# Moving the pre-work of the branch weights inside a hybrid mLSTM, attention and MLP layer, and the second branch's merges from GpSimd to VectorE

## The chip, the cores and the metric

The kernel runs on one core of a Trainium2 chip. The metric is the device time of one execution in microseconds (us), the median of several runs. Engines are named as in the profile: PE is TensorE, DVE is VectorE, ACT is ScalarE, POOL is GpSimd, and SP is the engine whose queue issues nearly all of this kernel's DMA transfers.

## The reference, cut to what matters

One decoder layer over 1024 positions of width 1024, in fp32. Three branches (mLSTM, differential attention, attention into 256 memory tokens) work on the normed input, each is projected back to 1024 columns and weighted by a gate, and the weighted sum goes through an output projection and an MLP.

```python
h = rms_norm(x, norm_mix_g[l])
proj = h @ w_in[l]
mq, mk, mv, mi, mf, mo, dq, dk, dv, cq = jnp.split(proj, split_idx, axis=-1)
qk = jax.nn.silu(causal_depthwise_conv(jnp.concatenate([mq, mk], axis=-1), conv_w[l], conv_b[l]))
mq, mk = jnp.split(qk, 2, axis=-1)
hm = mlstm_chunkwise(...)                # 4 heads of 128 x 256, chunks of 128 positions
y_m = jax.nn.sigmoid(mo) * rms_norm(hm, ...)
y_d = diff_attention(...)
y_c = memory_cross_attention(...)
g_m, g_d, g_c = jnp.split(jax.nn.sigmoid(h @ w_gate[l] + b_gate[l]), N_BRANCH, axis=-1)
merged = g_m * (y_m @ w_proj_m[l]) + g_d * (y_d @ w_proj_d[l]) + g_c * (y_c @ w_proj_c[l])
x = x + merged @ w_out[l]
h2 = rms_norm(x, norm_mlp_g[l])
x = x + jnp.square(jax.nn.relu(h2 @ w_up[l])) @ w_down[l]
```

## The kernel before

Every fp32 operand of a large product is split into a high and a low half of the matmul's own format, and each product is three matmuls. Splitting a tile is a cast (ACT) and a subtraction (DVE, lines 117 to 129). The gates, the branch projections and the MLP's first product are Winograd (Strassen) products: seven products of quarter size in place of eight, for which sums of the quarters of both operands are formed first.

The stages, in the order in which PE runs them (span times of the profile before): the input norm and the memory branch to about 190 us; the mLSTM stream to 560; differential attention to 1142; the gates to 1216.5; the three branch projections to 1456; the output projection to 1544; the MLP's up-projection and then its down-projection to the end.

**The mLSTM stream** is eight head halves (head 3 to 0, two halves of 512 positions each), a list of steps in which PE always has a projection to compute. A head half's own steps are: projection of q and k with the causal conv's four taps on DVE (lines 674, 678, 681; tiles `pre`, `cv`), values `va`, output gate `tho`, the mask tile `ngb` loaded and turned into a weight matrix `mpT`, then four chunks (`C` is the state, `Ch` its split for the next chunk's scores, `den` the denominators) and `final`, which scales the heads' output (`hS`, line 794) and transposes it. The chunks of one half run while the next half's q and k are being projected.

`early()` weaves extra work into that list, by positions: the sums of the branch projections' weights that the Winograd products want (tile `es`). `sums` is four DVE operations of 128x512 and four stores (to `ws`, or from the branch input `y` to `xc_d`); `pairs` is four DVE operations of 128x256, seven splits (an ACT cast and a DVE subtraction each) and seven stores to `wh`. Each first loads its four tiles. There are 8 pairs and 12 sums. Before, three sums stand at the stream's start, and from position 112 on pair and sums alternate every 49 positions, so that they fall anywhere in a head half, which is 64 positions long.

**The branch projections** (`branches()`) are 3 branches of 28 steps (7 products p of 4 steps kp), 12 matmuls each. The input of a step is split 5 steps ahead (tile `xs`), its weight is loaded 9 steps ahead (for the third branch from `wh`, already split). At the end of a product four PSUM tiles are evicted, partly through `te`, multiplied by a gate tile `gl` (loaded from `gates` in DRAM) and merged: branch 1 makes `mg`, branch 2 adds into `mg`, branch 3 adds `mg` and keeps the split result for the output projection. POOL does the merges of branch 2 (line 1611), part of those of branch 3 (line 1614), and sums and differences of the input's rows (`row`).

**Output projection and up-projection.** The output projection has four groups of four outputs; each output gets its residual in one DVE operation (line 1775, into a `gl` tile), is stored, and is squared into `ssq` by ACT and POOL (line 1782) for the next norm. It is also scaled (ACT, `h`) and stored to `h_d`, from where the up-projection loads its input `xr` in four parts `X[0]` to `X[3]`, forms the quarter sums (`xts`, lines 1274 to 1277) and splits them (`xo`). Its weights come as `wraw`, with sums by POOL (lines 1292 to 1295), and are split into `wo`.

The order on each engine is set by a scheduler at build time; `issue_after` and `behind` are hints to it that put an instruction behind another one without a semaphore. `self.hold` is such a mark for the first `wraw` loads.

Of the kernel before, what the change touches and what calls it, by code (L numbers as in the profile page):

```python
# [19 lines left out]
S = 1024  # L20
# [53 lines left out]
class Layer:  # L74
# [1249 lines left out]
    def wino(self, ws, load, use, first, parts):  # L1324
# [13 lines left out]
        X[2] = self.wino_x(2, load)  # L1338
# [91 lines left out]
    def early(self, pool, add):  # L1430
# [24 lines left out]
        def sums(p, srcs, dst, x):  # L1455
            t = []
            flat = lambda q: f32(q.rearrange("p a b -> p (a b)"))

            def load():
                t.extend(flat(new()) for _ in range(4))  # L1460
                return [nc.sync.dma_start(o, s) for o, s in zip(t, srcs)]

            def calc():
                t.extend([flat(new())] + ([None] * 2 if x else [t[1], t[2]]))
                return four(t, x)

            def store():
                r0, r1, r2, r3, e, f, g = t
                return [nc.sync.dma_start(dst[i], o) for i, o in enumerate((r0, r2, e, r3) if x else (r0, f, e, g))]

            at(p, load)
            at(p + 8, calc)
            at(p + 12, store)

        def pairs(p, b, kp, h):
# [19 lines left out]
            at(p, load)  # L1495
            at(p + 8, calc)
            for i in range(7):
                at(p + 10 + i, lambda i=i: cut(i))
                at(p + 13 + i, lambda i=i: keep(i))
# [3 lines left out]
        p = 2  # L1503
        for _ in range(3):
            sums(p, *S.pop(0))
            p += 17
        p = 112
        for n in range(8):
            pairs(p, 1, n // 2, n % 2)
            p += 29  # L1510
            sums(p, *S.pop(0))
            p += 20
        sums(p, *S.pop(0))
# [5 lines left out]
    def branches(self, pools, fetch, hi, lo):  # L1519
# [37 lines left out]
        def split(n, f):  # L1557
# [13 lines left out]
            if bi and p < 2:  # L1571
                r = lambda i: rows[bi, i, kp]
                if p == 0:
                    G.tensor_sub(r(1), r(2), r(0))
                else:
                    G.tensor_sub(r(3), r(3), r(1))

# [6 lines left out]
        def sums(bi, kp):  # L1584
            r = lambda i: rows[bi, i, kp]
            if bi == 1:
                t = op.tile([P, 512], F32, tag=("sq", "h2")[kp % 2], name=self.name("row"))
            else:
                t = xd.tile([P, 512], F32, tag="mh", name=self.name("row"))
            rows[bi, 4, kp] = t  # L1590
            G.tensor_sub(t, r(2), r(0))
            G.tensor_sub(r(0), r(0), r(1))
# [4 lines left out]
        def gate():  # L1597
            if outs:
                gates.append(fetch(self.gdr, *outs.pop(0)))

        mg, T, S = {}, {}, {}

        def out(bi, u, m, hf, c, late):
# [5 lines left out]
            elif bi == 1:  # L1609
                V.scalar_tensor_tensor(out=t, in0=t, scalar=1.0, in1=c, op0=ALU.add, op1=ALU.mult)  # L1610
                G.tensor_add(mg[ft, hf], mg[ft, hf], t)
            else:
# [3 lines left out]
                def keep():  # L1616
# [3 lines left out]
                    gate()  # L1620

                return keep
            gate()

        def evict(bi, p, u, ps):
# [7 lines left out]
            elif p in (1, 4):  # L1633
                V.tensor_add(T[u], T[u], ps)
                return out(bi, u, *((0, 1) if p == 1 else (1, 0)), T[u], False)
# [16 lines left out]
        for n in range(N):  # L1652
# [22 lines left out]
            for f in todo.pop(n, []):  # L1675
                k = f()
                if k:
                    if n < N - 1:
                        todo.setdefault(n + 2, []).append(k)
                    else:  # L1680
                        k()
# [11 lines left out]
        for n in sorted(todo):  # L1693
            for f in todo[n]:
                f()
        self.pinned = False
        self.hold = self.mark
# [25 lines left out]
    def tail(self):  # L1723
# [5 lines left out]
        def fetch(d, f, hf):  # L1729
            t = gls.tile([P, 512], F32, tag="gl", name=self.name("gl"))  # L1730
            nc.sync.dma_start(t, half(d, f, hf))
# [3 lines left out]
        with ExitStack() as c0:  # L1735
# [9 lines left out]
            with ExitStack() as c1:  # L1745
                E = lambda *x, **k: c1.enter_context(tc.tile_pool(*x, **k))
                self.pmm, self.kmm, self.nmm = Banks(E, "pmm2"), 8, 3
                if True:
# [10 lines left out]
                    V.memset(hole[:, 0:1], 0.0)  # L1759
                    V.memset(gap[:, 0:1], 0.0)  # L1760
# [8 lines left out]
                    for g in range(4):  # L1769

                        def res(m, hf, ps):
# [3 lines left out]
                            V.scalar_tensor_tensor(out=x, in0=ps, scalar=0.5, in1=x, op0=ALU.mult, op1=ALU.add)  # L1775
# [12 lines left out]
                        self.group(w, lambda k, i, hf: (lo if i else hi)[self.WOUT[k], hf], res, g == 0)  # L1788

# [446 lines left out]
```

## Time and profile before

| | |
|---|---|
| median of 3 runs | 2178.77 us (2174.14, 2178.77, 2179.9) |
| profiled execution | 2178.04 us, of which the span is 2176.2 |
| mean granted PE clock | 0.995 |
| busy: PE | 2117.4 us, 97% of the span |
| busy: DVE, ACT, POOL | 1556.2, 1055.3, 642.2 us |
| memory read and written | 214.15 MB and 98.60 MB, 144 GB/s over the span |

PE is busy nearly all the time, so what can be gained or lost in a change of order is PE's idle time, 58.8 us, and the time in which its clock is halved. A row of the profile names the line, the engine and the operation with its output and inputs; for a wait it names the instruction that ended it.

### The profile page before, as it was taken

What the parts mean: (1) busy time and instruction counts of PE and PEld (TensorE: products, weight loads), DVE (VectorE), ACT (ScalarE), POOL (GpSimd) and SP (SyncE); (2) the same over time, 40 slices, a digit from 0 to 9 for tenths busy, and PEclk for the clock granted to TensorE, in tenths of its full rate; (3) what the DMA queues carried; (4) which work ended last, traced back from release to release, by engine and by line L of the source; (5) the groups of instructions that cost most, each with busy time, mean ns of one, the idle gap of its engine ahead of it and who ended that gap; (6) DMA issues with size and microseconds to landing.
All of it is one profiled execution on the core that took longest, in us unless ns stands there. A gap on an engine that the chain in (4) does not pass through costs nothing.

```text
span 2176.2 us, 31507 instructions
## 1 busy us (share of the span) xinstructions
PE 2117.4 (97%) x10905; PEld 1829.7 (84%) x10905; DVE 1556.2 (72%) x2953; ACT 1055.3 (48%) x2183; POOL 642.2 (30%) x776
## 2 busy tenths in 40 slices
PE   7999999999999999999999999999899999999999
PEld 5888888888899999999887787788688888888887
DVE  6644677686647777777666588774578888876698
ACT  6543355454336666666554445334444544643331
POOL 2100000000111111111113054622455577665562
PEclk9999999999999999999999999999899999999999
DMA  6116456655343333333343885656434544844443
GB/s 242 42 67 207 132 190 211 198 184 174 138 154 90 86 86 89 90 95 88 97 150 112 300 273 158 228 194 220 136 112 150 208 155 156 294 161 154 159 160 107
DMA packets 183207, 340.00 MB, mean 156 GB/s; under 512 B 17633, under 2 KB 52742, under 8 KB 180998
## 3 DMA queue, kind: packets, MB, share of 16 engines
q1 hardware_dynamic: 176710, 318.05, 45.6%
q10 hardware_dynamic: 6336, 19.93, 2.3%
q8 instruction: 86, 1.41, 0.3%
q14 instruction: 75, 0.61, 0.1%
HBM read 214.15 MB, written 98.60 MB: 144 GB/s over the span
## 4 chain that ended last, share of the span: by engine, by line
PE 77%; DVE 9%; DMA 7%; ACT 2%; issue 2%; POOL 1%; SPq 0%; DVEq 0%; ACTq 0%; POOLq 0%
PE mm L96 30%; PE p L96 28%; PE mm L1668 7%; PE sc L96 5%; PE po L96 3%; PE tp L101 3%; DMA xr<-h_d 1%; DMA es<-in_wq 1%; DVE w L126 1%; DVE xs L69 1%; DVE cv L678 1%; DVE w L69 1%; DVE es L1451 1%; DMA raw<-in_wd 1%; PE pr L101 1%
## 5 line engine op out<-in xcount | busy, mean ns | idle before, releaser
L96 PE MATMUL mm<-w,hT 128*128 128x384 f32 (+3 forms) x2496 | 472.8, 332 | 5.7 <-DVE va L126 2.4
L96 PE MATMUL mm<-hT,w 128*128 128x512 f32 x1680 | 408.2, 393 | 0.3 <-ACT gt L503 0.3
L96 PEld LDWEIGHTS mm<-w,hT 128*128 128x128 f32 x2496 | 391.5, 190 | 17.2 <-DVE va L126 2.8
L96 PEld LDWEIGHTS mm<-hT,w 128*128 128x128 f32 x1680 | 308.2, 188 | 60.7 <-ACT gt L503 0.9
L96 PE MATMUL p<-xo,wo 128*128 128x512 f32 x1344 | 309.0, 392 | 1.6 <-DVE gl L1775 1.6
L96 PE MATMUL p<-xd,wo 128*128 128x512 f32 x1344 | 305.1, 389 | 0.0
L96 PEld LDWEIGHTS p<-xo,wo 128*128 128x128 f32 x1344 | 253.7, 189 | 55.6 <-DVE gl L1775 2.0
L96 PEld LDWEIGHTS p<-xd,wo 128*128 128x128 f32 x1344 | 252.2, 188 | 52.7 <-DVE acc L69 0.4
L1668 PE MATMUL mm<-xs,w 128*128 128x512 f32 x1008 | 231.4, 391 | 8.2 <-DMA w<-wh 4.7
L1668 PEld LDWEIGHTS mm<-xs,w 128*128 128x128 f32 x1008 | 190.0, 189 | 49.5 <-issue 5.1
L117 ACT CAST wo<-wraw 128x896 fp32r<-128x896 f32 x124 | 117.0, 944 | 230.2 <-PE p L96 87.3
L69 DVE TENSOR_TENSOR wo<-wraw,wo 128x896 fp32r<-128x896 f32 x124 | 148.5, 1209 | 47.0 <-ACT wo L117 47.0
L1292 POOL TENSOR_TENSOR wraw<-wraw 128x128 f32<-128x128 f32 x128 | 98.2, 767 | 229.9 <-DMA wraw<-in_wdown 95.2
L1041 ACT ACTIVATE dpe<-sc,dst,drr 128x256 f32<-128x256 f32 (+7 forms) x128 | 106.6, 833 | 97.0 <-DVE dst L1037 95.8
L126 DVE TENSOR_TENSOR w<-raw,w 128x256 fp32r<-128x256 f32 (+4 forms) x257 | 127.6, 521 | 28.1 <-ACT w L124 27.5
L124 ACT CAST w<-raw 128x256 fp32r<-128x256 f32 (+4 forms) x257 | 116.3, 488 | 48.2 <-PE mm L96 12.1
L151 POOL TENSOR_SCALAR hss<-hss 128x4 f32<-128x4 f32 x8 | 6.1, 765 | 429.7 <-ACT mscr L785 429.7
L1033 DVE CUSTOM_DVE_ANT_0 sc<-sc,tmask 128x256 f32<-128x256 f32 (+7 forms) x128 | 97.1, 759 | 13.1 <-PE sc L96 12.3
L151 POOL TENSOR_SCALAR drr<-drr 128x16 f32<-128x16 f32 x16 | 3.3, 204 | 311.8 <-DVE drr L988 289.8
L1294 POOL TENSOR_TENSOR wraw<-wraw 128x128 f32<-128x128 f32 x128 | 92.8, 725 | 0.0
L96 PE MATMUL sc<-dk,dq 128*128 128x512 f32 (+3 forms) x384 | 91.9, 347 | 0.0
L69 DVE TENSOR_TENSOR acc<-acc,p 128x512 f32<-128x512 f32 x121 | 80.1, 684 | 15.8 <-PE p L96 15.1
(333 smaller groups left out, 3496.9 us busy)
## 6 DMA issues: line engine op xcount, KB each, us to landing
dk<-dsg SPq DMA_DIRECT2D x64, 256.0 KB, 4.0
wraw<-in_wup SPq DMA_DIRECT2D x64, 256.0 KB, 3.1
r_d<-xts SPq DMA_DIRECT2D x16, 1024.0 KB, 4.5
wraw<-in_wdown SPq DMA_DIRECT2D x64, 256.0 KB, 3.1
wh<-es SPq DMA_DIRECT2D x56, 256.0 KB, 2.6
w<-wh SPq DMA_DIRECT2D x28, 512.0 KB, 4.1
raw<-in_wd SPq DMA_DIRECT2D x32, 384.0 KB, 3.3
gl<-gates SPq DMA_DIRECT2D x48, 256.0 KB, 3.4
```

The costliest lines, as they stand in the source:

```text
L69: return self.tc.keep_in_program_order(f(*a, **k))
L96: ins = self.nc.tensor.matmul(out, l, r, start=start, stop=stop)
L101: self.pin(self.nc.tensor.transpose(out, x, self.ident))
L117: self.cast = self.A.copy(hi, src).ins
L124: a = nc.scalar.copy(hi, src)
L126: return a, nc.vector.tensor_sub(lo, src, f32(hi))
L678: V.scalar_tensor_tensor(out=c, in0=x[:, q : q + 512], scalar=cw(q), in1=c, op0=ALU.mult, op1=ALU.add)
L1033: V.tensor_tensor_reduce(out=sc[:, 0:n], in0=sc[:, 0:n], in1=self.tmask[:, D - n : D], scale=1.0, scalar=-3.0e38, op0=ALU.add, op1=ALU.max ...
L1041: nc.scalar.activation(pe[c][:, 0:n], sc[:, 0:n], AF.Exp, bias=t8[:, 2 + c : 3 + c], scale=rr[:, i, c : c + 1], accum_out=t8[:, 4 + c : 5 ...
L1292: G.tensor_add(r[:, 4], r[:, 0], r[:, 3])
L1294: G.tensor_sub(r[:, 6], r[:, 1], r[:, 0])
L1668: nc.tensor.matmul(cur[u], w[:, l, c], x[:, m], start=first and i == 0, stop=last and i == 2, skip_group_check=True)
```

## The change

The work is the same, but for two DVE memsets that are dropped; where it is done differs.

1. `early()`: the pair of each head half comes at position 42 of the half, between its taps and its values' use (its loads 8 or 16 positions ahead). From the third head half on, two sums per half follow at 60 and 71 positions (the second one stands beside the first chunks of the half, at position 7 of the next). No sums are left at the start of the stream or in the first two head halves.
2. `branches()`: the 16 merges of branch 2 and the 4 of branch 3's product 1 go from POOL to DVE. The row sums on POOL are formed in another way, with as many operations, four of which come later. The load of a gate tile is issued a step later, and hinted behind the mark.
3. The up-projection's first `wraw` load is held until the output projection's second group (before: until the end of the branch projections), and the DVE part of `X[2]` is hinted behind the last residual operation of the output projection.

```diff
@@ early
             at(p, load)
-            at(p + 8, calc)
-            at(p + 12, store)
+            at(p + q, calc)
+            at(p + r, store)
...
-            at(p, load)
-            at(p + 8, calc)
+            at(p - (16 if p > 124 else 8), load)
+            at(p, calc)
             for i in range(7):
-                at(p + 10 + i, lambda i=i: cut(i))
-                at(p + 13 + i, lambda i=i: keep(i))
+                at(p + 1 + i, lambda i=i: cut(i))
+                at(p + 4 + i, lambda i=i: keep(i))
...
-        p = 2
-        for _ in range(3):
-            sums(p, *S.pop(0))
-            p += 17
-        p = 112
-        for n in range(8):
+        for n, p in enumerate((106, 124, 202, 266, 330, 394, 458, 522)):
             pairs(p, 1, n // 2, n % 2)
-            p += 29
-            sums(p, *S.pop(0))
-            p += 20
-        sums(p, *S.pop(0))
+            if n >= 2:
+                sums(p + 10, 8, 11, *S.pop(0))
+                sums(p + (22 if n < 7 else 18), 7, 9, *S.pop(0))
@@ branches
-            if bi and p < 2:
+            if bi and p < 3:
                 r = lambda i: rows[bi, i, kp]
                 if p == 0:
-                    G.tensor_sub(r(1), r(2), r(0))
-                else:
+                    G.tensor_add(r(1), r(1), r(4))
+                elif p == bi:
                     G.tensor_sub(r(3), r(3), r(1))
+                elif p == 1:
+                    G.tensor_sub(r(0), r(2), r(1))
...
             G.tensor_sub(t, r(2), r(0))
-            G.tensor_sub(r(0), r(0), r(1))
+            if bi == 1:
+                G.tensor_sub(r(0), r(0), r(1))
...
                 gates.append(fetch(self.gdr, *outs.pop(0)))
+                self.behind(self.fetched, self.mark)
...
-                G.tensor_add(mg[ft, hf], mg[ft, hf], t)
+                V.tensor_add(mg[ft, hf], mg[ft, hf], t)
...
-                return out(bi, u, *((0, 1) if p == 1 else (1, 0)), T[u], False)
+                return out(bi, u, *((0, 1) if p == 1 else (1, 0)), T[u], p == 1)
...
-                    todo.setdefault(n + 2, []).append(k)
+                    todo.setdefault(n + (1 if k is gate else 2), []).append(k)
...
-        self.hold = self.mark
@@ wino (up-projection)
-        X[2] = self.wino_x(2, load)
+        with self.tc.issue_after(self.last_stt):
+            X[2] = self.wino_x(2, load)
@@ tail
-                    V.memset(hole[:, 0:1], 0.0)
-                    V.memset(gap[:, 0:1], 0.0)
...
+                        if g == 1:
+                            self.hold = self.mark
```

PE's order is the same in both kernels. Three places show how the other orders move (numbers behind names are the program's; lines of the changed kernel are its own, 1452 for 1451, 1771 for 1775).

DVE in the sixth head half, before: the end, with the sums of `y` between the taps' last operations and `hS`.

```order
L681 SCALAR_TENSOR_TENSOR cv_5266<-cth_5271,cv_5266 128x512
L126 TENSOR_TENSOR w_6005<-raw_6003,w_6005 128x256
L1451 TENSOR_TENSOR es_5335<-es_5294,es_5292 128x512
L126 TENSOR_TENSOR kh_5274<-cv_5266,kh_5274 128x512
L1451 TENSOR_TENSOR es_5292<-es_5292,es_5293 128x512
L126 TENSOR_TENSOR va_1833<-mm_5320,va_1833 128x256
L1451 TENSOR_TENSOR es_5294<-es_5294,es_5292 128x512
L1451 TENSOR_TENSOR es_5295<-es_5295,es_5294 128x512
L794 TENSOR_SCALAR hS_5102<-hS_5102,hss_5103 128x256 x4
```

Before `hS` are four sums and, for the first of them, the landing of a load from `y`. The same stretch in the changed kernel:

```order
L126 TENSOR_TENSOR va_1832<-mm_5224,va_1832 128x256
L126 TENSOR_TENSOR w_5276<-raw_5274,w_5276 128x256
L794 TENSOR_SCALAR hS_5052<-hS_5052,hss_5053 128x256
L681 SCALAR_TENSOR_TENSOR cv_5213<-cth_5218,cv_5213 128x512
L794 TENSOR_SCALAR hS_5052<-hS_5052,hss_5053 128x256 x3
L126 TENSOR_TENSOR kh_5221<-cv_5213,kh_5221 128x512
L126 TENSOR_TENSOR w_5295<-raw_5274,w_5295 128x256
L126 TENSOR_TENSOR va_1833<-mm_5259,va_1833 128x256
```

The four `es` operations ahead of `hS` are gone. They stand earlier now, beside the first chunks of the same half, the last of the first sums and the first of the second:

```order
L1452 TENSOR_TENSOR es_4925<-es_4925,es_4924 128x512
L725 TENSOR_TENSOR ngb_5447<-ngb_5447,tmaskT 128x512
L126 TENSOR_TENSOR w_5046<-raw_5044,w_5046 128x256
L126 TENSOR_TENSOR w_5085<-raw_5044,w_5085 128x256
L773 SCALAR_TENSOR_TENSOR C_5064<-C_4653,g_dec,sc_5054 128x258
L126 TENSOR_TENSOR Ch_5066<-C_5064,Ch_5066 128x258
L781 TENSOR_TENSOR den_5069<-den_5069,g_col 128x1
L782 RECIPROCAL den_5069<-den_5069 128x1
L1452 TENSOR_TENSOR es_5091<-es_5030,es_5029 128x512
L773 SCALAR_TENSOR_TENSOR C_5106<-C_5064,g_dec,sc_5096 128x258
L1452 TENSOR_TENSOR es_5029<-es_5029,es_5032 128x512
L126 TENSOR_TENSOR Ch_5108<-C_5106,Ch_5108 128x258
```

Here the first `es` operation of the second sums (`es_5091`) stands ahead of the second chunk's `C`, and waits for loads that SP issues behind the four stores of the first sums. Before, a pair's subtractions (line 1489) stood around the first chunk's `C`:

```order
L1489 TENSOR_TENSOR es_4995<-es_4995 128x256
L773 SCALAR_TENSOR_TENSOR C_5114<-C_4704,g_dec,sc_5104 128x258
L1489 TENSOR_TENSOR es_5060<-es_5060 128x256
L126 TENSOR_TENSOR Ch_5116<-C_5114,Ch_5116 128x258
L781 TENSOR_TENSOR den_5119<-den_5119,g_col 128x1
L1489 TENSOR_TENSOR es_5061<-es_5061 128x256
L782 RECIPROCAL den_5119<-den_5119 128x1
L1489 TENSOR_TENSOR es_5062<-es_5062 128x256
L773 SCALAR_TENSOR_TENSOR C_5161<-C_5114,g_dec,sc_5151 128x258
L126 TENSOR_TENSOR Ch_5163<-C_5161,Ch_5163 128x258
```

The subtractions needed no load; the sums in their place do. POOL in the middle of branch 2, before: merges (line 1611) between sums of rows (lines 1574 and 1576).

```order
L1611 TENSOR_TENSOR mg_14424<-mg_14424,gl_15044 128x512
L1611 TENSOR_TENSOR mg_14429<-mg_14429,gl_15049 128x512
L1574 TENSOR_TENSOR row_14577<-row_14887,row_14787 128x512
L1611 TENSOR_TENSOR mg_14455<-mg_14455,gl_15074 128x512
L1611 TENSOR_TENSOR mg_14460<-mg_14460,gl_15079 128x512
L1574 TENSOR_TENSOR row_14600<-row_14909,row_14809 128x512
L1574 TENSOR_TENSOR row_14623<-row_14931,row_14831 128x512
L1574 TENSOR_TENSOR row_14649<-row_14957,row_14857 128x512
L1611 TENSOR_TENSOR mg_14527<-mg_14527,gl_15150 128x512
L1611 TENSOR_TENSOR mg_14531<-mg_14531,gl_15155 128x512
L1576 TENSOR_TENSOR row_14679<-row_14679,row_14577 128x512
```

Eight merges stand between the row operations that branch 3 needs. In the changed kernel, where the merges are on DVE:

```order
L1569 TENSOR_TENSOR row_14621<-row_14621,row_15081 128x512
L1569 TENSOR_TENSOR row_14647<-row_14647,row_15127 128x512
L1573 TENSOR_TENSOR row_14829<-row_14929,row_14621 128x512
L1573 TENSOR_TENSOR row_14855<-row_14955,row_14647 128x512
L1571 TENSOR_TENSOR row_14677<-row_14677,row_14571 128x512
L1571 TENSOR_TENSOR row_14699<-row_14699,row_14598 128x512
L1571 TENSOR_TENSOR row_14721<-row_14721,row_14621 128x512
L1571 TENSOR_TENSOR row_14749<-row_14749,row_14647 128x512
L1613 TENSOR_TENSOR gl_15488<-mg_14314,gl_15488 128x512
```

POOL has only the row operations left, up to the first merge of branch 3 (line 1613).

DVE at the end of the output projection, before: the three `xts` operations of `X[2]` stand ahead of three residual operations and the splits of two weights (`wo`).

```order
L1775 SCALAR_TENSOR_TENSOR gl_16396<-mm_16371,gl_16396 128x512
L1274 TENSOR_TENSOR xts_16681<-xr_16679 128x512
L1276 TENSOR_TENSOR xts_16681<-xr_16679,xts_16681 128x512
L1277 TENSOR_TENSOR xts_16681<-xr_16679,xts_16681 128x512
L1775 SCALAR_TENSOR_TENSOR gl_16431<-mm_16406,gl_16431 128x512
L1775 SCALAR_TENSOR_TENSOR gl_16466<-mm_16441,gl_16466 128x512
L126 TENSOR_TENSOR wo_16697<-wraw_16661,wo_16697 128x7x128
L69 TENSOR_TENSOR wo_16734<-wraw_16691,wo_16734 128x7x128
L1775 SCALAR_TENSOR_TENSOR gl_16501<-mm_16476,gl_16501 128x512
```

The residual operations behind them wait for `xr`, the landing of `X[2]`. In the changed kernel:

```order
L1771 SCALAR_TENSOR_TENSOR gl_16394<-mm_16369,gl_16394 128x512
L1771 SCALAR_TENSOR_TENSOR gl_16429<-mm_16404,gl_16429 128x512
L1771 SCALAR_TENSOR_TENSOR gl_16464<-mm_16439,gl_16464 128x512
L126 TENSOR_TENSOR wo_16695<-wraw_16659,wo_16695 128x7x128
L69 TENSOR_TENSOR wo_16732<-wraw_16689,wo_16732 128x7x128
L1771 SCALAR_TENSOR_TENSOR gl_16499<-mm_16474,gl_16499 128x512
L1274 TENSOR_TENSOR xts_16679<-xr_16677 128x512
L126 TENSOR_TENSOR xo_16684<-xr_16677,xo_16684 128x3x512
L1276 TENSOR_TENSOR xts_16679<-xr_16677,xts_16679 128x512
L1277 TENSOR_TENSOR xts_16679<-xr_16677,xts_16679 128x512
```

All four residual operations of the last group now stand ahead of `X[2]`.

More of the change, by code (lines that the diff above doesn't have):

```diff
@@ L1453, in early, with sums @@
         new = lambda: pool.tile([P, 2, 256], F32R, tag="w", name=self.name("es"))
-        def sums(p, srcs, dst, x):
+        def sums(p, q, r, srcs, dst, x):
             t = []
@@ L1619, in keep @@
                     self.split2(hi[ft, hf], lo[ft, hf], t)
-                    gate()
+                    return gate
                 return keep
-            gate()
+            return gate
         def evict(bi, p, u, ps):
@@ L1676, in branches @@
                 k = f()
+                while k and n == N - 1:
+                    k = k()
                 if k:
-                    if n < N - 1:
-                        todo.setdefault(n + 2, []).append(k)
-                    else:
-                        k()
+                    todo.setdefault(n + (1 if k is gate else 2), []).append(k)
             if n + LEAD < N + 4:
@@ L1694, in branches @@
             for f in todo[n]:
-                f()
+                while f:
+                    f = f()
         self.pinned = False
-        self.hold = self.mark
         return w0
@@ L1730, in fetch @@
             t = gls.tile([P, 512], F32, tag="gl", name=self.name("gl"))
-            nc.sync.dma_start(t, half(d, f, hf))
+            self.fetched = nc.sync.dma_start(t, half(d, f, hf)).ins
             return t
@@ L1774, in res @@
                             x = fetch(a["xT"], f, hf)
-                            V.scalar_tensor_tensor(out=x, in0=ps, scalar=0.5, in1=x, op0=ALU.mult, op1=ALU.add)
+                            self.last_stt = V.scalar_tensor_tensor(
+                                out=x, in0=ps, scalar=0.5, in1=x, op0=ALU.mult, op1=ALU.add
+                            ).ins
                             nc.sync.dma_start(half(self.x1d, f, hf), x)
```

## The prediction

> **What bounds the kernel now.** I read the profiled execution first by engine, then by stage, then by PE's waits in each stage.
>
> ```profile
> PE 2117.4 (97%) x10905; PEld 1829.7 (84%) x10905; DVE 1556.2 (72%) x2953; ACT 1055.3 (48%) x2183; POOL 642.2 (30%) x776
> 190.00:560.00 370.00, 353.69 (x2081) 311.34 (x2080) 260.71 (x685) 180.42 (x510) 13.86 (x14) 0.99 0.58 189
> 1216.50:1456.00 239.50, 231.26 (x1009) 190.04 (x1008) 187.49 (x229) 104.04 (x186) 95.72 (x65) 0.99 0.69 229
> 1456.00:1544.00 88.00, 87.16 (x385) 71.84 (x385) 44.65 (x55) 32.32 (x47) 27.12 (x21) 1.00 0.64 208
> 1544.00:1562.00 18.00, 9.18 (x40) 7.18 (x38) 11.01 (x10) 8.46 (x10) 9.26 (x8) 0.82 0.46 157
> ```
>
> The last four rows are stretches of the span: length, then busy time of PE, its weight loads, DVE, ACT and POOL, then PE's granted clock. PE bounds everything; PE's order does not change, so the change can only give back or add PE's idle time and the time at a lower clock. Length less busy PE is 16.3 us of idle in the mLSTM stream, 8.2 in the branch projections, 0.8 in the output projection, 8.8 at the up-projection's start: 34.1 us within reach of the change. The other 24.7 of PE's 58.8 idle us lie at the start, in attention, the gates and the MLP, which it does not touch.
>
> The clock comes on top. Four stretches ran at half clock; behind two of them I put one of equal length just after:
>
> ```profile
> 453.16:456.57 3.41, 3.41 (x18) 3.41 (x18) 3.17 (x9) 0.00 (x0) 0.00 (x0) 0.50 0.91 224
> 457.50:460.91 3.41, 3.41 (x31) 3.36 (x30) 2.98 (x7) 1.69 (x5) 0.00 (x0) 1.00 0.77 270
> 500.95:504.36 3.41, 3.41 (x17) 3.25 (x17) 1.21 (x4) 1.09 (x2) 0.00 (x0) 0.50 0.59 190
> 1391.83:1395.24 3.41, 3.41 (x8) 2.69 (x9) 0.00 (x0) 0.00 (x0) 0.50 (x1) 0.50 0.96 365
> 1397.00:1400.41 3.41, 3.41 (x17) 2.83 (x16) 1.30 (x2) 0.68 (x2) 0.00 (x0) 1.00 0.73 215
> 1555.67:1569.32 13.65, 8.70 (x29) 7.45 (x29) 5.11 (x4) 6.87 (x10) 11.83 (x19) 0.50 0.60 200
> ```
>
> 18 matmuls where 31 fit: 13/31 of 3.41 us lost, 1.4 us. The second, by the same pace, 1.4. The third 9/17 of 3.41, 1.8. The fourth did 29 in 8.70 busy us; at 17 in 3.41 it would have done 43, so 14/43 of 8.70, 2.8 us. Together 7.4 us.
>
> **The mLSTM stream: what goes.** PE's waits there:
>
> ```profile
> PE tp L101 <- DVE hS L794: 7.3, 4, 4.4
> PE mm L96 <- DVE va L126: 2.4, 2, 1.8
> ...
> PE sc L96 <- ACT Ch L124: 1.9, 2, 1.5
> ...
> PE sc L96 <- DVE Ch L126: 1.0, 3, 0.4
> ```
>
> Columns: total us, times, longest. DVE's own order shows who stands ahead at the longest `hS` and `va`:
>
> ```profile
> 449.51 0.76 DVE L1489 TENSOR_TENSOR es<-es 128x256 fp32r<-128x256 f32 x2
> ...
> 451.45 0.42 DVE L126 TENSOR_TENSOR va<-mm,va 128x256 fp32r<-128x256 f32 x1
> ...
> 496.79 0.69 DVE L1451 TENSOR_TENSOR es<-es,es 128x512 f32<-128x512 f32 x1 [1.73 <-DMA es<-y]
> ...
> 498.94 1.41 DVE L1451 TENSOR_TENSOR es<-es,es 128x512 f32<-128x512 f32 x2
> 500.26 1.14 DVE L794 TENSOR_SCALAR hS<-hS,hss 128x256 f32<-128x256 f32 x4
> ```
>
> At `hS` it is 1.73 us of waiting for a load and four sums, 2.8 us: 4.5, about the 4.4 us that PE stood. So `es` operations in DVE's queue make the stalls. In the changed order none stand before the third head half except two pairs, and later none between the taps and `hS`. I count 15.3 of the 16.3 us as gone (1.0 kept for the short `Ch` waits) and the two half-clock stretches, 2.8: 18.1 us.
>
> The clock needs a rule here, since both stretches follow a stall within 3 to 5 us. The first comes after a stall of 1.8 us, the row of `va`. The Trainium skill, "TensorE: Matmul & The Clock Gate", section "Why this matters for your kernels", asks only that PE have no idle gap over about 3 us; by it the first stretch would not be there, and this trace disagrees. By that page new stalls under 3 us would cost no clock; the sum would not move, as I charge them none either.
>
> **The mLSTM stream: what comes in.** The pair at position 42 has only `tho` and splits around it, before values are needed 14 positions later; seven subtractions and four sums are 11 x 0.4 us (the rows at 449.51 and 451.45 show that size), spread over as many positions: hidden. Its loads are put ahead on SP, where the mask tile `ngb` is queued; DVE waits for that tile before the change too. The first sums stand after `mpT`, ahead of nothing that PE needs soon: hidden too. The second sums are the price. Their four loads sit on SP behind the four stores of the first sums, and their first operation stands ahead of the second chunk's `C` on DVE, on which `Ch` and PE's next scores hang.
>
> ```profile
> L1461 SPq DMA_DIRECT2D es<-in_wq x32: 422/430/686, 194.4 to 420.5; - x32
> L1469 SPq DMA_DIRECT2D ws<-es x32: 319/327/1014, 201.7 to 428.6; - x32
> DMA to landing us min/median/max: 2.0/3.4/6.8
> DVE es L1451 <- DMA es<-in_wq: 7.7, 7, 2.8
> ```
>
> From the end of the first sums: four stores at 0.33, two loads at 0.43 and a landing of 3.4 make 5.6 us until the first operation can run (4.2 with the shortest landing, 9.0 with the longest). The stream's 370 us for eight halves make a head half at most 46 us and a position of 64 at most 0.7; the second chunk follows the first by 4 positions, 2.8 us, and the first sums end about a position ahead of the first chunk, so DVE is there 3 to 4 us after them. It then waits about 2 us (0 to 5.5). How much of it reaches PE the trace does not show. Below it is nothing; above, the nearest row is the 4.4 us at `hS`, where a 1.73 us wait met the end of a full queue. Here one 0.68 us operation and not four stands between, and `Ch` has a chunk's 2.8 us to run in, so I take 1.2 us per half, nearer to zero. Six halves have such sums: 7.2 us (0 to 26). Net gain in the stream 10.9.
>
> **The branch projections.** PE's waits, and what SP waits for:
>
> ```profile
> PE mm L1668 <- DMA w<-wh: 4.7, 1, 4.7
> PE mm L1668 <- DVE xs L69: 2.0, 2, 1.7
> PE mm L1668 <- DVE hole L1759: 1.6, 1, 1.6
> SPq L1731 <- POOL mg L1611: 36.0, 16, 6.1
> 1379.61 3.52 POOL L1611 TENSOR_TENSOR mg<-mg,gl 128x512 f32<-128x512 f32 x2
> 1379.61 7.49 DVE L69 TENSOR_TENSOR xs<-row,xs 128x512 fp32r<-128x512 f32 x5
> ```
>
> The weight that came late was queued on SP behind gate loads (line 1731), which wait for a `gl` tile that POOL's merge still reads, and POOL was behind with merges and row sums. With the merges on DVE right behind the multiplication, and the load a step later, that wait (4.7 and its 1.8 of clock) goes. The `xs` waits (2.0) have the other half of the cause: beside POOL, DVE's splits took 1.5 us each (7.49 for five) where the sums above take 0.68. Less POOL work means faster splits. The 1.6 us at the stage's start stay: there DVE is busy with the last gate's sums, and dropping a memset takes away a name, not the work. Gain 4.7 + 1.8 + 2.0 = 8.5 us.
>
> The price is 20 additions on DVE, 20 x 0.68 = 13.6 us on an engine that is busy 187.5 of 239.5 us; against that, 20 POOL operations of about 1.7 us no longer slow the splits. I cost it at nothing; the cover is the five steps of lead, 12 matmuls each: 239.5 us / 84 = 2.85 us a step, 14 us.
>
> The Trainium skill, "SBUF — State Buffer", section "SBUF: two separate sides", says that DVE and GpSimd share a port pair as an exclusive lock: a DVE operation with two SBUF inputs is blocked while a GpSimd one holds it. The rows above (1.5 against 0.68 us) agree. By it the new DVE merges, which have two SBUF inputs, would be caught too wherever POOL still sums rows; that is the slower rival below, worked out from rows there.
>
> **The output projection's end.**
>
> ```profile
> 1537.86 7.65 DMA xr<-h_d
> ...
> 1545.60 0.69 DVE L1274 TENSOR_TENSOR xts<-xr 128x512 f32<-128x512 f32 x1 [12.99 <-DMA xr<-h_d]
> 1545.64 1.80 POOL L1275 TENSOR_TENSOR xts<-xr 128x512 f32<-128x512 f32 x1 [9.57 <-DMA xr<-h_d]
> 1548.64 1.28 DVE L1775 SCALAR_TENSOR_TENSOR gl<-mm,gl 128x512 f32<-128x512 f32 x2
> 1549.38 3.71 PE L96 MATMUL p<-xo,wo 128*128 128x512 f32 x15 [1.59 <-DVE gl L1775]
> 1550.12 2.55 POOL L1782 TENSOR_TENSOR ssq<-ssq,sq 128x512 f32<-128x512 f32 x2 [2.68 <-ACT sq L1781]
> 1555.50 1.69 PE L96 MATMUL px<-ones,ssq 128*128 128x1 f32 x8 [2.42 <-DVE gl L1775]
> 1557.01 0.45 POOL L1292 TENSOR_TENSOR wraw<-wraw 128x128 f32<-128x128 f32 x1 [4.34 <-DMA wraw<-in_wup]
> 1558.78 3.31 POOL L1782 TENSOR_TENSOR ssq<-ssq,sq 128x512 f32<-128x512 f32 x1
> 1562.14 1.87 PE L96 MATMUL px<-ones,ssq 128*128 128x1 f32 x8 [4.95 <-POOL ssq L1782]
> ```
>
> DVE stood 13 us on the landing of `X[2]` with finished PSUM tiles behind it. Put behind the last residual, `X[2]` no longer holds them: 1.59 and 2.42 go. The last `ssq` addition comes late because POOL has a weight's sums ahead of it, whose load landed only at 1557. In the new order the split that frees its buffer stands behind residuals that are done early, so the load goes out several us sooner; but POOL's `xts` of `X[2]` still waits for 1545.5, and two `ssq` additions, four weight sums and the last addition follow: 1.8 + 2.6 + 1.8 + 1.3 to 3.3 us, ready at 1553 to 1555, where PE, without its 4.0 us of waits, comes to the first `px` at 1551.5 and to the second, which needs the addition, 1.7 later (the two lie 1555.5 and 1562.1 now). I keep 2.5 us of stall, the late end: 6.5 us of the 9.0 go (0 to 9), and 1.8 of the 2.8 us of clock, since a 2.5 us gap may still cost one stretch. Late next is `X[3]`: its load waits for the last `h` store, and its landing (7.7 us for `X[2]`) and splits end about when PE needs them, near 1572; 1.0 us for that (0 to 4). Net 7.3. The 0.8 us ahead of the output projection I leave.
>
> **Sum.** 10.9 + 8.5 + 7.3 = 26.7 us off the profiled 2178.04 (span 2176.2 and 1.8 around it): 2151.3. The median of the runs lies 0.7 above that execution: 2152.
>
> **The rivals.**
> - *The second sums stall every half.* For it: DVE already waited 2.8 us once for such a load with nothing queued ahead on SP. Against it: only PE's slack on `Ch` decides. At 2.8 us a stall and a half-clock stretch (1.4) each time, six halves cost 25.2 instead of 7.2: 2170. At the bound of 4.4 with clock, 34.8: 2180, and all is lost.
> - *DVE becomes the bound in branch 2, slower.* Eight of the merges fall into two successive products. If POOL's row sums catch a product's 12 two-input operations at 1.5 us, and its other 8 take 0.68, the product needs 23.4 us where PE needs 11.4. Two in a row are 24 us late, less 14 of lead: 10 us. Twice in branch 2 and once in branch 3, each with a clock loss of 1.8, that is 35, and the 8.5 us gained are gone: 2195. It decides from the point where the lateness of successive products passes 14 us. Against it: the row sums fill POOL only part of the time, and DVE idles 52 us here.
> - *The gate loads still block SP.* The hint on them adds no semaphore, and if POOL's row sums stay late the weight is too: 6.5 us kept, 2158.5.
> - *The gain at the output projection's end is handed back* at `X[3]` or `ssq`: 2158.
>
> **How the numbers follow.** Forecast 0.58 (its own range 2144 to 2161, from new stalls of 0 to 2.5 us a half and the up-projection's 0 to 9), stalls in every half 0.17 (a quarter of this near no change), DVE bound 0.07, SP still blocked 0.09, handed back 0.09. Range 2140 to 2171. No change is within 0.3%, 6.5 us, about what runs of this kernel tell apart (they spread over 5.8). Faster 0.86: all but the DVE rival and the worst end of the first. Same 0.07, slower 0.07.
>
> **What would show it.** Right: no `hS` wait over 1 us and no half clock in the stream; no `w<-wh` wait on PE, and SP's waits on line 1731 far below 36 us; splits `xs` near 0.7 us in branch 2; no `gl` wait at the up-projection's start. Wrong: `Ch` waits on PE six times behind DVE waiting for `es` loads; `xs` waits on PE in branch 3's first products; a wait for `xo` near 1572.

## The result and the profile after

The changed kernel takes 2156.86 us (median; 2153.97 to 2159.72) against 2178.03 for the kernel before in the same comparison: a ratio of 0.9905 with a 95% interval of 0.9884 to 0.9926, some 21 us (16 to 25). The profiled execution took 2153.97 us, its span 2151.7.

PE executes the same instructions in the same order in both kernels. So the start of one and the same matmul in the two traces tells how far ahead the changed kernel is there. This ledger shows where the time came from; how far two traces of one order can differ is told below, with the experiments:

| matmul | starts before, us | starts after, us | ahead, us |
|---|---|---|---|
| first head half, first scores (`sc<-va,mpT`) | 259.73 | 260.07 | -0.3 |
| its state update (`sc<-va,ks`) | 262.97 | 266.50 | -3.5 |
| last stalled scores of the stream (`sc<-Ch,qp`) | 530.20 | 520.78 | 9.4 |
| attention (`mm<-w,hT`) | 614.48 | 603.97 | 10.5 |
| branch projections, after their first wait | 1219.62 | 1208.41 | 11.2 |
| first step of branch 3 that waited for `wh` | 1391.78 | 1373.15 | 18.6 |
| first of the output projection (`mm<-ml,w`) | 1457.27 | 1436.07 | 21.2 |
| first `px` | 1555.50 | 1530.22 | 25.3 |
| second `px` | 1562.14 | 1536.18 | 26.0 |
| end of the span | 2176.2 | 2151.7 | 24.5 |

About 10 us come from the mLSTM stream, 10.7 from there to the output projection (10.0 of them in the branch projections behind their first wait), 4.8 from there to the second `px`. Some 1.5 us are given back in the MLP, with no wait that names them.

The stages of the changed kernel, at the bounds where PE passes from one to the next (columns as in the prediction):

```profile
190.00:549.10 359.10, 351.34 (x2078) 309.83 (x2077) 253.51 (x669) 177.95 (x502) 11.78 (x14) 0.99 0.56 182
1205.90:1434.70 228.80, 227.77 (x1005) 188.26 (x1004) 186.79 (x246) 104.03 (x183) 61.77 (x41) 1.00 0.72 238
1434.70:1523.02 88.32, 88.32 (x391) 72.81 (x389) 47.58 (x58) 35.02 (x51) 28.83 (x25) 1.00 0.67 214
1523.02:1540.00 16.98, 11.80 (x52) 9.84 (x51) 8.71 (x9) 7.09 (x8) 12.05 (x16) 0.79 0.64 213
```

PE's idle time fell from 16.3 to 7.8 us in the stream, from 8.2 to 1.0 in the branch projections, from 0.8 to nothing in the output projection, and from 8.8 to 5.2 at the up-projection's start. PE's waits say what is left there:

```profile
PE px L96 <- POOL ssq L1780: 4.9, 1, 4.9
PE sc L96 <- ACT mpT L124: 3.1, 1, 3.1
...
PE sc L96 <- DVE Ch L126: 2.2, 4, 1.2
...
PE sc L96 <- ACT Ch L124: 1.4, 3, 0.7
...
PE mm L1667 <- DVE u L1261: 1.0, 1, 1.0
```

The waits on `hS`, `va`, `tho` and `gf` are gone or at 0.3 us, and so is the one on `wh`. Three things remain: the first head half's `mpT`, which did not wait before; short waits on `Ch`; and `px`, which waits for `ssq` as long as before. Two of them bring a half-clock stretch, in the first head half and at `px`:

```profile
259.66:266.49 6.83, 6.42 (x16) 5.03 (x17) 4.06 (x10) 3.25 (x10) 0.00 (x0) 0.50 0.65 220
1532.83:1543.07 10.24, 6.89 (x20) 5.83 (x21) 4.85 (x5) 5.14 (x8) 10.01 (x14) 0.50 0.59 195
```

### The profile page after: what moved, and what is told of

Read it like the earlier page. It is cut to its first block, busy times and chain, and to the rows that moved or that the text cites. A ratio compares the mean times of both kernels' runs of the same rounds, so it can differ in the third digit from the quotient of the medians.

```text
span 2151.7 us, 31481 instructions
## 1 busy us (share of the span) xinstructions
PE 2112.8 (98%) x10905; PEld 1827.4 (85%) x10905; DVE 1559.6 (72%) x2971; ACT 1057.0 (49%) x2183; POOL 615.1 (29%) x756
## 3 DMA queue, kind: packets, MB, share of 16 engines
q8 instruction: 86, 1.41, 0.3%
## 4 chain that ended last, share of the span: by engine, by line
PE 75%; DVE 8%; DMA 8%; ACT 3%; issue 2%; SPq 1%; POOL 1%; DVEq 0%; ACTq 0%; POOLq 0%
PE mm L96 27%; PE p L96 26%; PE mm L1667 11%; PE sc L96 5%; PE po L96 3%; PE tp L101 2%; DMA es<-in_wq 2%; DVE w L126 1%; DVE es L1452 1%; DVE cv L678 1%; DMA xr<-h_d 1%; SPq L1462 1%; PE pr L101 1%; DMA es<-y 1%; DMA wraw<-in_wdown 1%
## 5 line engine op out<-in xcount | busy, mean ns | idle before, releaser
L1292 POOL TENSOR_TENSOR wraw<-wraw 128x128 f32<-128x128 f32 x128 | 101.1, 790 | 214.2 <-DMA wraw<-in_wdown 101.0
L1294 POOL TENSOR_TENSOR wraw<-wraw 128x128 f32<-128x128 f32 x128 | 96.9, 757 | 0.0
```

The costliest lines, as they stand in the source:

```text
L1292: G.tensor_add(r[:, 4], r[:, 0], r[:, 3])
L1294: G.tensor_sub(r[:, 6], r[:, 1], r[:, 0])
```

## The experiments

Times are medians. The experiments were run in several series, each with its own runs of the kernel before, whose medians lay between 2178 and 2183 us, so kernels of different series are compared by their ratios to it (the changed kernel: 0.9905, 0.9884 to 0.9926). "By PE's events" means the ledger's method: the start of one and the same matmul in two traces.

**The pre-work back in its old places.**

```diff
-        for n, p in enumerate((106, 124, 202, 266, 330, 394, 458, 522)):
...
+        p = 2
+        for _ in range(3):
+            sums(p, *S.pop(0))
+            p += 17
...
```

> The changed kernel with the pre-work of the branch weights placed as before; all else as changed. By PE's events the changed kernel is 10 us ahead when the mLSTM stream ends. Theory (the stalls of the stream hang on where that work stands): these 10 us go, about 2167 us, with the waits on hS, va and tho and the two half-clock stretches back. Rival (the stream's gain is mostly luck of when loads land): less than 4 us is lost, and a part of the waits stays away.

2166.67 us, ratio 0.995 (0.9931 to 0.997), about 10 us lost. PE's waits in the stream:

```profile
PE tp L101 <- DVE hS L794: 7.2, 4, 3.9
PE sc L96 <- ACT Ch L124: 4.5, 4, 1.9
PE mm L96 <- DVE gf L648: 2.8, 3, 1.4
PE mm L96 <- DVE va L126: 2.4, 2, 1.8
```

The waits on `hS` and `va` are back as they were, those on `Ch` and `gf` are longer than before, and `tho` waits 0.6 us. Half clock is back too, in three stretches of 3.41 us. The stream's gain hangs on where the pre-work stands; the rival of luck is out. By PE's events the loss at the stream's end is 15 us and not 10: this trace is 6 us behind that of the kernel before there, with the same order on every engine up to that point.

**The merges of branch 2 back on POOL.**

```diff
-                V.tensor_add(mg[ft, hf], mg[ft, hf], t)
+                G.tensor_add(mg[ft, hf], mg[ft, hf], t)
```

> The changed kernel with the 16 merges of branch 2 back on POOL; gate loads a step later and the row sums as changed. Theory (the merges on POOL hold gl tiles, and with them SP's queue and DVE's splits): 7 to 10 us are lost, about 2165 us, with the w<-wh wait on PE of some 4 us back and xs splits near 1 us. Rival (the later gate loads alone free SP): less than 2 us is lost and no w<-wh wait.

2165.57 us, ratio 0.9945 (0.9923 to 0.9967): some 9 us lost, in the trace 12 within the branch projections. SP's and PE's waits in the branch projections:

```profile
SPq L1729 <- POOL mg L1610: 41.8, 16, 10.2
...
PE mm L1667 <- DMA w<-wh: 9.0, 1, 9.0
```

The wait on `wh` is back, longer than before. POOL's merges hold the gate tiles, these hold SP's queue, and the queue holds the weight. The splits `xs` take 1048 ns here, as they did before (1046).

**The gate loads as before.**

```diff
-                self.behind(self.fetched, self.mark)
...
-                    return gate
+                    gate()
...
-            return gate
+            gate()
```

> The changed kernel with the gate loads issued as before (a step earlier, with no hint); merges on VectorE. Theory of the merges: within 2 us of the changed kernel, no w<-wh wait. Rival of the gate loads: SP is held by gl again, the w<-wh wait returns, 4 to 7 us lost.

2155.43 us, ratio 0.99 (0.9873 to 0.9927); by PE's events within 1 us of the changed kernel everywhere, and no wait on `wh`. The later loads and the hint are worth nothing that can be measured. Without the merges of branch 2 on DVE nothing is gained in this stage. Whether the row sums' new form and the four merges of branch 3 add to it was not tested.

**`X[2]` without its hint.**

```diff
-        with self.tc.issue_after(self.last_stt):
-            X[2] = self.wino_x(2, load)
+        X[2] = self.wino_x(2, load)
```

> The changed kernel without the hint that puts VectorE's part of X[2] behind the last residual. PE's events gave 4.5 us to the end of the output projection. Theory (VectorE stands on X[2] with finished tiles behind it): 4 us are lost, two waits on gl of 1.5 to 2.5 us return. Rival (ScalarE's wait for an h store and the weight load behind it set this place either way): at most 1 us is lost.

2157.09 us, ratio 0.9908 (0.9884 to 0.9932). PE's waits at that place:

```profile
PE px L96 <- POOL ssq L1779: 3.4, 1, 3.4
PE px L96 <- DVE gl L1770: 2.1, 1, 2.1
```

One wait on `gl` returned, as the theory had it, but what it costs the wait on `ssq` loses: 5.5 us together, 5.2 in the changed kernel. The theory fell. The hint alone is worth nothing that can be measured there: the second `px` waits for `ssq` either way.

**The hold back, and hold and hint both back.**

```diff
-                        if g == 1:
-                            self.hold = self.mark
...
+        self.hold = self.mark
```

> The changed kernel with the first wraw load held until the end of the branch projections, as before; X[2]'s hint kept. The hint alone was worth nothing. Theory (the earlier weight load is what brought the 4.5 us at the end of the output projection): the two waits of px come to 8 us or more and 3 to 4.5 us are lost. Rival (either of the two suffices): less than 1.5 us is lost.

> The changed kernel with both the hold and X[2]'s hint as before. Theory (the earlier weight load alone): like the run with the hold alone put back, within 1 us at PE's second px. Rival (either suffices): 4 us are lost only here, with waits on gl and ssq of 8 to 9 us together.

With the hold back: 2161.33 us, ratio 0.9911 (0.9895 to 0.9928). With both: 2162.76, ratio 0.9912 (0.989 to 0.9933). Waits from the output projection on, first with the hold back, then with both:

```profile
PE px L96 <- POOL ssq L1781: 4.9, 1, 4.9
PE mm L96 <- DVE ml L69: 0.8, 1, 0.8
```

```profile
PE px L96 <- POOL ssq L1780: 5.3, 1, 5.3
PE px L96 <- DVE gl L1771: 1.6, 1, 1.6
```

The hold is worth the 0.8 us of `ml` at the output projection's first matmul, which I had left standing, and nothing at `px`. With both back the waits of `px` come to 6.9 us, and by PE's events the run loses 1.9 us against the changed kernel between the output projection and the second `px`. So either of the two suffices at `px`, as the rival had it, but for 2 us and not 4. The ledger has 4.8 us there. The other 2.9 stay open: from the output projection to behind the second `px`, the run with both back has the same order on every engine and on SP as the kernel before, so the order there is not what they come from.

**The first pair's loads earlier.** In the changed kernel one of these four loads stands on SP ahead of `g_dec`, which waits for a store, and three stand between `g_dec` and the mask tile:

```profile
242.68 0.45 SPq L1482 DMA_DIRECT2D es<-in_wq  x1
246.79 0.33 SPq L588 DMA_DIRECT2D g_dec<-g_dd  x1
247.16 2.61 SPq L1482 DMA_DIRECT2D es<-in_wq  x3
249.87 0.38 SPq L721 DMA_DIRECT2D ngb<-g_dng  x1
...
254.50 0.69 DVE L725 TENSOR_TENSOR ngb<-ngb,tmaskT 128x512 f32<-128x512 f32 x1 [5.33 <-DMA ngb<-g_dng]
```

Before, the same two instructions stood at 245.58 and 250.20:

```profile
245.58 0.45 SPq L721 DMA_DIRECT2D ngb<-g_dng  x1
...
250.20 0.69 DVE L725 TENSOR_TENSOR ngb<-ngb,tmaskT 128x512 f32<-128x512 f32 x1 [0.47 <-DMA ngb<-g_dng]
```

`ngb` is issued 4.3 us later, and with it `mpT` and PE's first scores, in a kernel that was 2.9 us ahead until then. Before, `g_dec` stood behind `ngb` (at 247.68); now SP stands on `g_dec` until 246.79 and then issues three loads, 2.6 us, ahead of `ngb`.

```diff
-            at(p - (16 if p > 124 else 8), load)
+            at(p - (8 if p == 124 else 16), load)
```

> The changed kernel with the first pair's four loads 8 positions earlier, so that they stand on SP ahead of the g_dwi, g_dng and g_dd group and not between it and the mask tile ngb. Theory (these loads, stuck behind g_dec's wait on SP, held up ngb and by it PE's first scores by 3.1 us and 6.8 us of half clock): that wait goes, 5 to 6.5 us less, about 2151 us. Rival (ngb is late for its own data): the 3 us wait stays, less than 1 us gained.

2148.16 us, ratio 0.9857 (0.9835 to 0.9879). The `mpT` wait is gone, and so is the half clock in the stream; by PE's events the kernel is 6.2 us ahead of the changed one at the first state update (the ledger's second row), 4.6 when attention begins and 5.9 at the end of the span. `ngb` is issued ahead of `g_dec` again, at 242.97. So the run takes away `g_dec`'s wait and the three loads together, and doesn't tell which weighs more.

**The second sums later.** In the last head half of the changed kernel DVE stands on a load of the second sums, and the chunk's `C` and `Ch` stand behind it:

```profile
517.64 0.69 DVE L1452 TENSOR_TENSOR es<-es,es 128x512 f32<-128x512 f32 x1 [4.09 <-DMA es<-y]
518.25 0.48 DVE L773 SCALAR_TENSOR_TENSOR C<-C,g_dec,sc 128x258 f32<-128x258 f32 x1
518.65 0.69 DVE L1452 TENSOR_TENSOR es<-es,es 128x512 f32<-128x512 f32 x1
...
520.31 0.42 DVE L126 TENSOR_TENSOR Ch<-C,Ch 128x258 fp32r<-128x258 f32 x1
```

```diff
-                sums(p + (22 if n < 7 else 18), 7, 9, *S.pop(0))
+                sums(p + (22 if n < 7 else 18), 7 + 5 * (n < 7), 9 + 5 * (n < 7), *S.pop(0))
```

> The changed kernel with the second sums of each head half 5 positions later, behind the third chunk's C on VectorE and no longer ahead of the second's. Theory (the waits on Ch, 3.6 us in all, are the price of second sums that wait for their loads): they fall under 1 us, 2 to 3 us gained in the stream. Rival (the same operations among the taps hold up hS and va in turn): hS or va waits of 2 us or more, nothing gained or a loss.

2149.14 us, ratio 0.9858 (0.9839 to 0.9877). The `Ch` waits fell from 3.6 us to this, and `hS` waits 0.3 us:

```profile
PE sc L96 <- ACT Ch L124: 0.7, 2, 0.4
```

By PE's events the kernel is 0.4 us ahead of the changed one behind the first head half (270 us), 7.1 at the stream's end and 5.5 when attention begins, where the waits make up 2.9: more than expected, and the rest has no wait that names it.

**A third buffer for `h`, and the last `ssq` addition first.** Why does `px` still wait? In the changed kernel's chain of waits stands a store of `h`:

```profile
1517.12 7.79 DMA h_d<-h
```

and behind its landing, on ACT, DVE and POOL:

```profile
1524.99 0.72 ACT L1782 ACTIVATE h<-gl,vec 128x512 f32<-128x512 f32 x1 [5.74 <-DMA h_d<-h]
1525.62 0.93 ACT L124 CAST wo<-wraw 128x896 fp32r<-128x896 f32 x1
...
1526.58 1.89 DVE L126 TENSOR_TENSOR wo<-wraw,wo 128x896 fp32r<-128x896 f32 x1 [8.06 <-ACT wo L124]
...
1531.51 1.14 POOL L1292 TENSOR_TENSOR wraw<-wraw 128x128 f32<-128x128 f32 x1 [3.99 <-DMA wraw<-in_wup]
...
1534.87 1.26 POOL L1780 TENSOR_TENSOR ssq<-ssq,sq 128x512 f32<-128x512 f32 x1
```

ACT needs a buffer for `h`, and the store that frees it takes 7.8 us, issued just behind the 1 MB load of `X[2]`. Behind `h` on ACT waits the split of `wo`, behind that the next weight load, and behind that, on POOL, the sums that stand ahead of the last addition.

```diff
-                            h = op.tile([P, 512], F32, tag="h2", name=self.name("h2"))
+                            h = gap if (f, hf) == (7, 0) else op.tile([P, 512], F32, tag="h2", name=self.name("h2"))
```

> The changed kernel with a third buffer for one of the last two scaled outputs h, so that ScalarE need not wait for the store of an earlier one (it stood 5.7 us on it, behind a transfer of 1 MB). Theory (this wait holds up wo, the weight load behind it, the weight sums and ssq): the px wait shrinks from 4.9 to under 2 us, 3 to 5 us gained. Rival (POOL would still be late, since X[2]'s xts waits for its landing): under 1 us.

2159.5 us, ratio 0.9908 (0.9889 to 0.9927), no gain. PE's waits there:

```profile
PE p L96 <- DVE wo L69: 3.2, 1, 3.2
PE px L96 <- POOL ssq L1780: 3.0, 1, 3.0
```

`px` waits 1.9 us less, but the weight's split comes late instead. With this edit the scheduler also changed the order on ACT, DVE, POOL and SP at the output projection's end, so the run does not show the buffer by itself. Then the other way, on POOL itself:

```diff
+        if late:
+            self.behind(first.ins, late)
+            self.behind(second.ins, late)
...
+                self.wino_s(r, getattr(self, "last_ssq", None) if n >= 4 else None)
```

> The changed kernel with the weight sums on POOL from the fifth weight on put behind the last ssq addition. Theory (the 4.9 us wait of px is POOL's queue: a late weight load and four sums stand ahead of a ready addition): px waits 1 us or less, 4 us and some 2 us of half clock gained, about 2151 us. Rival (VectorE's xo split then takes the shared port and the addition still ends late, or the weight sums come late in turn and PE waits for wo): under 2 us gained.

2158.24 us, ratio 0.9898 (0.9878 to 0.9918): as a whole, no gain that can be measured. At the place:

```profile
PE px L96 <- POOL ssq L1783: 1.0, 1, 1.0
PE p L96 <- DVE wo L69: 0.8, 1, 0.8
```

The wait fell as expected. The trace was 5.5 us behind the changed kernel's at 1134 us, where the two kernels' orders do not differ, and 1.7 at the second `px`, so 3.8 us are gained between. The 5.5 us are what one order of instructions varies by from run to run; seven of the kernels here have the same order up to that place, and their traces reach it up to 6.8 us apart. A single trace shows waits, not a time to 5 us.

**The fixes together.**

> The changed kernel with the first pair's loads 8 positions earlier and the second sums 5 positions later. Theory (two separate causes in the stream, each worth 5 us by PE's events): their gains add, no wait over 1 us is left in the stream, about 2147 us. Rival (both stalls cover the same slack): no better than one of them, 2150 to 2152 us.

With the pair earlier and the second sums later: 2141.77 us, ratio 0.9814 (0.9799 to 0.9829). PE's only wait in the stream that the trace names:

```profile
PE tp L101 <- DVE hS L794: 0.2, 1, 0.2
```

By PE's events it is 12.5 us ahead of the changed kernel when attention begins (alone, the two were 4.6 and 5.5 ahead) and 11.3 at the end of the span. By the ratios it is some 20 us faster than the changed kernel, where each alone was 10: the two gains add, and come out larger than expected.

> As the kernel with the earlier pair and the later second sums, and the last ssq addition ahead of the weight sums on POOL. Theory: another 3 to 4 us, about 2143 us, px waits 1 us, of which a wo wait of about 1 us comes back. Rival (the time is handed to the wait on wo): within 1 us of that kernel.

With the `ssq` addition first as well: 2140.36 us, ratio 0.981 (0.9795 to 0.9824), the fastest kernel of this study, 1% below the changed one by the ratios, whose intervals do not overlap. Against the kernel with two fixes the times differ by 1.4 us, too little to be told from nothing; in the trace the second `px` comes 4.1 us earlier, no half-clock stretch is left before the last microseconds, and 1.7 of it go to a new wait:

```profile
PE p L96 <- ACT pt L1385: 1.7, 1, 1.7
...
PE px L96 <- POOL ssq L1783: 0.6, 1, 0.6
```

## Why the prediction was right, and where a step failed

The forecast was 2152 us, a gain of 26.7 us; 21 us were measured in the medians and 24.1 in the profiled execution. What bounds the kernel, the sign and the two large sources hold. That the sum came so near is in part luck: the stream's gain and its new costs were both larger than forecast, and nearly cancel. Of the signs of being right three did not come: half clock stayed in the stream, `xs` did not come near 0.7 us, and SP's waits on the gate loads are not far below 36 us. Of the signs of being wrong, the `Ch` waits came in part. By its own steps:

- *The stream, net 10.9.* The ledger says 10, and undoing the change there costs 10 by the medians. The two halves of that number were each off. What went was more than the 18.1 forecast: with both new costs taken out, attention begins 23 us ahead of before (10.5 and 12.5).
- *The pair at position 42 "hidden".* This is the step that failed. I saw its loads ahead of `ngb` on SP and priced them at nothing, since DVE waits for that tile anyway; that `ngb` would also fall behind `g_dec` and its wait I did not see. In the first head half DVE's wait was only 0.47 us, so most of the delay of 4.3 us went on to PE: 3.1 us of wait and a half-clock stretch, 6.4 us by PE's events (2.9 ahead before it, 3.5 behind after it). The trace of before had the 0.47; I did not read the wait half by half. (The second pair, too, stands in the first head half, at position 60 of it, and not at 42 of its own.)
- *The second sums, 7.2.* The mechanism is right: DVE waits for their loads with `C` behind it, 4.09 us in the row above. Moving them on was worth 5.5 us at attention's begin. The waits on `Ch` come in four halves, 3.6 us together, and not six times 1.2.
- *The branch projections, 8.5.* 10.0 by the ledger with the 0.8 of `ml`, 9 lost when the merges alone go back: right. The cause inside was half wrong. The later gate load, which I named beside the merges, is worth nothing. And the splits did not come near 0.7 us: the groups are, before and after,

```profile
L69 DVE TENSOR_TENSOR xs<-row,xs 128x512 fp32r<-128x512 f32 x56 | 58.1, 1046 | 25.8 <-ACT xs L117 25.7
```

```profile
L69 DVE TENSOR_TENSOR xs<-row,xs 128x512 fp32r<-128x512 f32 x56 | 51.3, 929 | 16.6 <-ACT xs L117 16.6
...
L69 DVE TENSOR_TENSOR mg<-mg,gl 128x512 f32<-128x512 f32 x16 | 13.6, 848 | 0.5
```

  929 ns against 1046: POOL still works beside some of them. Taken one by one, the splits with no POOL operation at the same time take 0.69 us in both traces; those that overlap one take 1.41 us before and 1.44 after, and there are 18 of them where there were 28. The 16 merges take 848 ns on DVE where 680 were assumed (five of them overlap a POOL operation, at 1.19 us), so the slower rival's mechanism is there, at a fifth of the price it would need. DVE's total did not grow in this stage (186.8 us against 187.5): the additions make 16.2 us, and the splits and multiplications beside them are shorter by as much. SP's waits for gate tiles (line 1729, before 1731) are now on DVE, 45.4 us in all against 61.8, of which POOL had 36.0; the longest on a merge is 3.7 us and was 6.1, and no weight is late.
- *The 1.6 us at the stage's start stay.* They do: 1.0 us here, 0.8 to 1.7 in the other runs.
- *The output projection's end, 7.3.* 4.8 by the ledger. I kept 2.5 us of stall on `px` (my own late end, 1555 against 1551.5 and 1.7, gives 1.8); it is 4.9. The step that failed: "the load goes out several us sooner". It does, against the up-projection's first matmul: 5.5 us after it (1528.50 and 1523.02) where it was 9.6 (1553.78 and 1544.22). But PE is at `px` 3.8 us sooner too, so the stall stays. My sum had POOL working without a pause from `xts` on; in the row above it stands 3.99 us on this load, and the four sums behind it take 3.4 us where I had 1.8. I had freed the load of its wait on DVE and did not look at ACT, where the same split stands behind `h`, whose buffer waits for a store. X[2]'s hint as such gained nothing. The rival that this gain is handed back named the place, `ssq`; `X[3]` was not late.

## What to carry to other kernels

A load that is moved ahead of another on a queue is priced at the tightest of the waits behind it, one by one, never at their sum or mean: seven of eight pairs brought no such wait, and the first cost 6 us. What already waits between the two on the queue belongs into that price. Work whose inputs come by DMA belongs behind the operation that another engine waits for, not ahead of it, even when the average landing leaves time. And when a wait that was removed costs the same under a new name, follow the chain one engine further back before buying a buffer: reordering the last consumer removed the wait, and in the run with the buffer it came back under another name.

## What the hardware showed

The clock fell after waits far below 3 us, and neither the longest wait nor the sum of two decides. In the last head half two waits on `Ch` follow each other. In the run without `X[2]`'s hint they are 1.08 and 1.17 us, and PE goes on at full clock:

```profile
519.99 0.38 PE L96 MATMUL sc<-Ch,qp 128*128 128x258 f32 x1 [1.08 <-ACT Ch L124]
521.54 0.51 PE L96 MATMUL sc<-Ch,qp 128*128 128x258 f32 x2 [1.17 <-DVE Ch L126]
```

In the run with the third buffer they are 1.08 and 1.18 us, and half clock follows at 521.12:

```profile
519.92 0.38 PE L96 MATMUL sc<-Ch,qp 128*128 128x258 f32 x1 [1.08 <-ACT Ch L124]
521.47 0.80 PE L96 MATMUL sc<-Ch,qp 128*128 128x258 f32 x2 [1.18 <-DVE Ch L126]
```

The stretches of half clock quoted in this document last 3.41, 6.83, 10.24 or 13.65 us, one to four times 3.41, and within a trace they begin and end on one grid of that step: from 266.49 to 1532.83 in the changed kernel are 371 steps of 3.413. In the first of the two runs this grid, carried on from its half clock at 260.80, has a bound at 520.21, between the two waits; in the second it has one at 521.12, near the end of the second wait. The stretches of the grid, first without the hint, then with the third buffer:

```profile
516.80:520.21 3.41, 2.33 (x14) 1.84 (x12) 1.81 (x4) 0.69 (x4) 0.00 (x0) 1.00 0.35 133
520.21:523.62 3.41, 2.24 (x11) 1.79 (x11) 3.41 (x9) 1.38 (x6) 0.00 (x0) 1.00 0.72 277
```

```profile
517.71:521.12 3.41, 1.50 (x9) 1.04 (x7) 2.78 (x6) 1.38 (x5) 0.00 (x0) 1.00 0.29 112
521.12:524.53 3.41, 3.06 (x8) 2.59 (x9) 3.41 (x9) 1.42 (x5) 0.00 (x0) 0.50 0.54 206
```

PE is idle 1.08 and 1.17 us in the first two, and 1.91 us in the one ahead of the half clock. In all fourteen traces, from 20 us on to 5 us before the end, each of the 27 stretches of the grid at full clock in which PE idles 1.79 us or more is followed by half clock; with less, down to 1.03 us, both happen. The Trainium skill, "TensorE: Matmul & The Clock Gate", section "What's actually happening", gives a free-running window of 3413 ns; the lengths agree with it, and the waits above would fit a gate that counts busy time within such a window. No run here varied the place of a wait alone, so it stays an explanation.

A 256 KB store took 7.8 us to land when it was issued 0.9 us after a 1 MB load on the same queue, against 2.4 us for the one before it (1517.12 and 1513.71 in the chain of waits). It is one case, and no run took the load away.
